# From which SBUF pool the operand tiles of the down projection's products come

## The chip, the cores and the metric

The kernel runs on one core of a Trainium2 chip. The metric is the device time of one execution in microseconds (us); the forecast and the result go by the median of several runs. One further execution was recorded by the hardware profiler, and all views of the profile come from it.

## What is computed

One decoder block over 1,024 tokens of width 1,024 in float32: three attention branches and their merge, then a squared-ReLU MLP. The change lies in the MLP's second product, the way down:

```python
h2 = rmsnorm(x, g_mlp_norm[l])
u = jax.nn.relu(jnp.einsum('bsd,df->bsf', h2, w_ff_up[l]))     # 1024 x 4096
x = x + jnp.einsum('bsf,fd->bsd', u * u, w_ff_down[l])         # 4096 -> 1024, the way down
```

## The kernel before

**Precision.** Each float32 operand is split into a high part (a copy rounded to the type of TensorE's operands, made by ACT) and a low part (the rest, by a subtraction on DVE). A product of two operands is three matmuls: high by high, high by low, low by high.

**The way down, lines 2509 to 2692.** The product of 1,024 x 4,096 by 4,096 x 1,024 is done by a scheme of seven block products in place of eight (`DOWN`: P1, P2, P6, P7, P5, P4, P3). The inner dimension comes in four groups of 4 x 128 pairs; the seven products of each group make 28, numbered k = 0 to 27 in `plan`. The left-hand operand of a product (128 partitions x 4 x 512) has been written to DRAM by the way up (`s_scr`) and is loaded into a "ur" tile by `load_s`. The right-hand one is a block of `w_down` (tiles w11, w12, w21, w22, loaded by `load_wb`) or a difference of such blocks (t1 to t4), taken on DVE by `right_sum`.

Each product k has 48 matmuls of 128 x 128 by 128 x 512 (line 2660): four token tiles t, four slices c, three passes. In a pass the left-hand operand is the stationary one (`sop[k]`: `sh`, `sl`) and the right-hand operand the moving one (`top[k]`: `th`, `tl`). Of the eight banks of PSUM, products of kind P1, P6, P5 and P3 use four (tags pp, pp, pp, pv), the others four (sc, sc, tr, tr).

**Order of the work.** It is written out by hand in the loop of line 2652; nothing reorders it. While product k runs, the operands of k+1 are made: behind the matmuls of t = 0 the right-hand sum and high part (`right(k+1, 0)`, ACT line 2575), behind t = 1 the right-hand low part (DVE) and the left-hand high part (`left(k+1, 0)`, ACT line 2588), behind t = 2 the left-hand low part (DVE). Between them stand the additions of finished PSUM banks to the output tiles (`out_evict`; on DVE, in group 0 partly ACT copies, line 2645). `load_s(k + 2)` and the next group's weight loads go out on SP's queue. DVE's `tensor_tensor` is called in the helper `tt`, line 1919, so all its rows have that line; tiles tell them apart.

**Pools.** A tile of 4 x 512 float32 numbers takes 8,192 bytes of each partition. Pool `RA` stands on the right-hand side of SBUF and has four places with the tag "h" (and one each of g0 to g3, which hold w21, w12, w22 and w11). Pool `V` stands on the left-hand side and has six places with the tag "sop", three with "ur" and one for each of t1 to t4. A pool hands out the places of a tag in turn, and whoever writes a place again waits for the last reader of the tile that was there. `operand(RA)` (line 1945) takes two h places, `vt("sop", F32R)` one sop place. In the program as laid out, the h places begin at byte 163,712 + 8,192 n of each partition, n = 0 to 3, and the sop places at 42,752 + 8,192 n, n = 0 to 5.

Before the change, product 0 has all four operand tiles in h places (`pieces["u"]`, `pieces["w"]`, made at the end of the way up), product 1 all four in sop places, and each later product its right-hand pair in h and its left-hand pair in sop. `parts` (line 2563) makes the operands of product 2 in two halves.

Of the kernel before, what the change touches and what calls it, by code (L numbers as in the profile page):

```python
# [15 lines left out]
F32R = mybir.dt.float32r  # L16
# [22 lines left out]
def f32(ap):  # L39
    return ap.bitcast(F32)  # L40
# [3 lines left out]
def tile_hybrid_block(  # L44
# [260 lines left out]
    RA = Pool("ra", side="right", h=4, g0=1, g1=1, g2=1, g3=1)  # L305
# [1553 lines left out]

    OUT = ("P1", "P2", "P6", "P5", "P3", "P7", "P4")  # L1860
    left, right, ring = {}, {}, {}

    def wtile(tag, dt):
# [54 lines left out]
    def tt(out_, a_, b_, op):  # L1918
        nc.vector.tensor_tensor(out_, a_, b_, op)  # L1919
# [25 lines left out]
    def operand(pool, tag="h"):  # L1945
        return tuple(pool.t(tag, [P, 4, 512], F32R) for _ in range(2))

    xm = []
    for s in range(0, ST, 2):
        t = RA.t("h", [P, 2, D])  # L1950
# [93 lines left out]
    with tc.manual_schedule():  # L2044
# [288 lines left out]
        def parts(hi, lo, raw):  # L2333
            yield Op("ACT", act_time(1024), lambda: nc.scalar.activation(hi, raw, AF.Copy))
            yield Op("DVE", dve_time(1024), lambda: tt(lo, raw, f32(hi), ALU.subtract))
# [182 lines left out]
        def vt(tag, dt=F32):  # L2518
            if tag in side_of:
                return RA.t(side_of[tag], [P, 4, 512], dt)  # L2520
            return laid.pop(tag) if tag in laid else V.t(tag, [P, 4, 512], dt)
# [4 lines left out]
        wb, sraw, sop, top = {}, {}, {}, {}  # L2526

        def load_wb(j, tag, queue_=nc.sync):
            if j < len(groups):
                p, n_ = groups[j]  # L2530
                wb[j, tag] = vt(tag)[:, :n_]
                rows = w_down[2 * p * P:2 * (p + n_) * P, :].rearrange("(c i p) n -> i p c n", i=2, p=P)
                dh = int(tag[2]) - 1
                queue_.dma_start(wb[j, tag], rows[int(tag[1]) - 1][:, :, dh * 512:(dh + 1) * 512])

        def load_s(k, queue_=nc.sync):
            if k < len(plan):
# [3 lines left out]
                r0 = (DOWN.index(kind) * NP + p) * P  # L2541
                queue_.dma_start(sraw[k], s_scr[r0:r0 + n_ * P, :].rearrange("(c p) n -> p c n", p=P))

        def right_sum(k):

            j, kind = plan[k]
            n_ = groups[j][1]
            if kind == "P6":
                r = wb[j, "t2"] = vt("t2")[:, :n_]
                tt(r, wb[j, "w22"], wb[j, "t1"], ALU.subtract)  # L2550
            elif kind == "P7":
                r = wb[j, "t3"] = vt("t3")[:, :n_]
                tt(r, wb[j, "w22"], wb[j, "w12"], ALU.subtract)
                load_wb(j + 1, "w12")
            elif kind == "P4":
                r = wb[j, "t4"] = vt("t4")[:, :n_]
                tt(r, wb[j, "w21"], wb[j, "t2"], ALU.subtract)
                load_wb(j + 1, "w21")
            else:
                r = wb[j, {"P1": "w11", "P2": "w21", "P5": "t1", "P3": "w22"}[kind]]  # L2560
            return r
# [5 lines left out]
        def right(k, part):  # L2567
            j, kind = plan[k]
            n_ = groups[j][1]
            if part == 0:  # L2570
                raw = right_sum(k)
                h_, l_ = operand(RA) if k > 1 else (vt("sop", F32R), vt("sop", F32R))
                top[k] = h_[:, :n_], l_[:, :n_], raw
                for cs in parts(k):
                    nc.scalar.activation(top[k][0][:, cs], raw[:, cs], AF.Copy)  # L2575
            else:
                h_, l_, raw = top[k]
                for cs in parts(k):
                    tt(l_[:, cs], raw[:, cs], f32(h_[:, cs]), ALU.subtract)
                if kind == "P3":  # L2580
                    load_wb(j + 1, "w22")

        def left(k, part):
            n_ = groups[plan[k][0]][1]
            if part == 0:
                sop[k] = vt("sop", F32R)[:, :n_], vt("sop", F32R)[:, :n_]
                for cs in parts(k):
                    nc.scalar.activation(sop[k][0][:, cs], sraw[k][:, cs], AF.Copy)  # L2588
            else:
                for cs in parts(k):  # L2590
                    tt(sop[k][1][:, cs], sraw[k][:, cs], f32(sop[k][0][:, cs]), ALU.subtract)
# [60 lines left out]
        for k, (j, kind) in enumerate(plan):  # L2652
            n_ = groups[j][1]
            for t in range(4):
# [9 lines left out]
                if k == 1 and t == 2:  # L2664
                    left(k + 1, 1)
# [4 lines left out]
                if k + 1 < len(plan):  # L2670
                    if t == 0:
                        right(k + 1, 0)
                    elif t == 1:
                        right(k + 1, 1)
                        left(k + 1, 0)
                    elif t == 2 and k != 1:
                        left(k + 1, 1)
# [46 lines left out]
```

## Time and profile before

| | |
|---|---|
| median of 3 runs | 1685.87 us (1685.17 to 1685.92) |
| the profiled execution | 1685.24 us |
| its span, first to last instruction | 1683.5 us |
| granted TensorE clock | 1.0 |
| way down: first weight load of product 0 to first of product 27 | 1366.10 to 1667.88 us |
| DVE, one operation on 128 x 2048 there | 2.29 us |
| ACT, one copy of 128 x 2048 there | 1.9 us |

In the views, PE is TensorE's matmuls and PEld its weight loads, DVE VectorE, ACT ScalarE, POOL GpSimd and SP the queue of SyncE. Tiles go by their tags: `pp<-h,sop` is a matmul into a bank pp with an h tile as moving and a sop tile as stationary operand. The weight load of a matmul begins about when the matmul before it begins; a matmul's own duration in the records (some 390 ns) is longer than its distance to the next, since matmuls overlap, so the pace is read from the distance of starts. The row that joins n weight loads gives the time from the start of the first to the end of the last.

### The profile page before, as it was taken

Reading aid. Unit: us, or ns where it says so; the run is one execution under the profiler, and the core shown is the slowest. Engines: PE = TensorE matmul, PEld = TensorE weight load, DVE = VectorE, ACT = ScalarE, POOL = GpSimd, SP = SyncE. Lnnn points to the kernel's source line nnn. Section 1 sums busy time; section 2 is a strip of 40 time slices with the busy share of each in tenths; the row PEclk is TensorE's granted clock in tenths of the full one; section 3 lists DMA queues with packets and bytes.
Section 4 is the critical chain, followed back from the end, with each engine's and each line's share of the span. In section 5 each row is a group of like instructions: output and inputs, shape, how many; then the busy total and the mean of one; then the engine's idle time right before and its main releaser. Section 6 shows DMA issues by size and latency. Waiting matters only on the chain.

```text
span 1683.5 us, 25003 instructions
## 1 busy us (share of the span) xinstructions
PE 1672.9 (99%) x9118; PEld 1431.8 (85%) x9118; DVE 1292.8 (77%) x2079; ACT 848.8 (50%) x1474; POOL 255.1 (15%) x440
## 2 busy tenths in 40 slices
PE   9999999999999999999999999999999999999999
PEld 9998899998888888888888887878888888888887
DVE  7977778855459888877877898987777776688775
ACT  6455555535458888876761446432333344332331
POOL 0000000000153142254400011022111120000000
PEclk9999999999999999999999999999999999999999
DMA  6445434467374354477747542144443485553532
GB/s 245 156 152 179 153 118 145 139 196 254 117 241 147 128 172 150 134 243 223 234 147 244 180 167 101 55 160 155 156 151 137 151 300 183 201 204 138 198 125 76
DMA packets 142221, 284.32 MB, mean 169 GB/s; under 512 B 16913, under 2 KB 53329, under 8 KB 142098
## 3 DMA queue, kind: packets, MB, share of 16 engines
q1 hardware_dynamic: 110562, 183.08, 31.8%
q0 software_dynamic: 31536, 99.64, 18.8%
q8 instruction: 72, 1.18, 0.3%
q14 instruction: 51, 0.42, 0.1%
HBM read 189.83 MB, written 92.83 MB: 168 GB/s over the span
## 4 chain that ended last, share of the span: by engine, by line
PE 93%; DVE 4%; DMA 1%; ACT 1%; issue 1%; SPq 0%; DVEq 0%; ACTq 0%
PE pp L1458 11%; PE pp L1146 10%; PE pp L1983 10%; PE pp L2660 8%; PE sc L1458 7%; PE sc L1146 6%; PE sc L1983 5%; PE sc L2660 4%; PE tr L2660 4%; PE tr L919 4%; PE pv L1458 3%; PE pv L2660 3%; PE tr L1983 2%; PE sc L936 2%; PE pp L936 2%; DVE h L1919 1%
## 5 line engine op out<-in xcount | busy, mean ns | idle before, releaser
L1057 DVE TENSOR_TENSOR wlo<-raw,whi 128x1024 fp32r<-128x1024 f32 (+1 forms) x88 | 107.5, 1221 | 80.4 <-ACT whi L1056 80.1
L1056 ACT ACTIVATE whi<-raw 128x1024 fp32r<-128x1024 f32 (+1 forms) x88 | 93.2, 1059 | 78.8 <-PE pp L1458 32.7
L2660 PE MATMUL pp<-h,sop 128*128 128x512 f32 x540 | 128.4, 395 | 0.0
L2660 PEld LDWEIGHTS pp<-h,sop 128*128 128x128 f32 x540 | 101.4, 188 | 24.6
L1983 PE MATMUL pp<-h,oh 128*128 128x512 f32 x384 | 120.6, 395 | 0.7 <-ACT cu L2068 0.6
L926 DVE TENSOR_TENSOR ptl<-tr,pth 128x512 fp32r<-128x512 f32 (+1 forms) x160 | 99.1, 628 | 24.1 <-ACT pth L924 23.4
L924 ACT ACTIVATE pth<-tr 128x512 fp32r<-128x512 f32 (+1 forms) x160 | 87.4, 557 | 34.8 <-PE sc L936 15.4
L1983 PEld LDWEIGHTS pp<-h,oh 128*128 128x128 f32 x384 | 72.1, 188 | 18.4 <-ACT cu L2068 1.5
L2575 ACT ACTIVATE h<-t 128x2048 fp32r<-128x2048 f32 (+1 forms) x17 | 30.8, 1815 | 109.4 <-DVE t L1919 96.6
L1375 POOL DMA_DIRECT2D raw<-w_in x32 | 24.2, 755 | 396.2 <-DVE wlo L1057 396.2
L1458 PE MATMUL pp<-h,whi 128*128 128x512 f32 x248 | 77.7, 394 | 0.0
L1146 PE MATMUL sc<-h,whi 128*128 128x512 f32 (+1 forms) x254 | 77.1, 387 | 0.0
L1983 PE MATMUL pp<-h,ol 128*128 128x512 f32 x192 | 75.8, 395 | 0.0
L1458 PE MATMUL pp<-whi,h 128*128 128x256 f32 x384 | 72.1, 283 | 0.0
L845 DVE TENSOR_TENSOR_SCAN e<-r,e 128x384 f32<-128x384 f32 (+3 forms) x64 | 66.3, 1044 | 7.0 <-ACT e L830 6.6
L1976 ACT ACTIVATE oh<-raw 128x512 fp32r<-128x512 f32 x64 | 39.4, 624 | 62.0 <-DVE raw L1919 62.0
L2660 PE MATMUL sc<-h,sop 128*128 128x512 f32 x264 | 63.4, 395 | 0.0
L2660 PE MATMUL tr<-h,sop 128*128 128x512 f32 x264 | 63.4, 395 | 0.0
L1919 DVE TENSOR_TENSOR sop<-ur,sop 128x2048 fp32r<-128x2048 f32 (+1 forms) x28 | 61.8, 2209 | 1.7 <-ACT sop L2588 1.7
L919 PE MATMUL tr<-ident,e 128*128 128x128 f32 x416 | 62.5, 273 | 0.0
L1458 PEld LDWEIGHTS pp<-whi,h 128*128 128x128 f32 x384 | 60.4, 189 | 0.0
L2660 PEld LDWEIGHTS tr<-h,sop 128*128 128x128 f32 x264 | 49.6, 188 | 12.0
(558 smaller groups left out, 5085.0 us busy)
## 6 DMA issues: line engine op xcount, KB each, us to landing
ur<-s_scr SPq DMA_DIRECT2D x26, 1024.0 KB
raw<-w_in POOLq DMA_DIRECT2D x42, 512.0 KB, 5.0
raw<-w_up SPq DMA_DIRECT2D x60, 256.0 KB
s_scr<-s POOLq DMA_DIRECT2D x60, 256.0 KB, 2.6
g<-w_down SPq DMA_DIRECT2D x14, 1024.0 KB
s_scr<-cu POOLq DMA_DIRECT2D x48, 256.0 KB, 2.8
h<-sbk_scr POOLq DMA_DIRECT2D x64, 128.0 KB, 3.0
o<-gate_scr SPq DMA_DIRECT2D x32, 256.0 KB
```

The lines of the kernel that those rows point to most:

```text
L845: nc.vector.tensor_tensor_scan(out=back, data0=rho[:, :u][:, ::-1], data1=back, initial=0.0 if last else beta[:, c + u:c + u + 1], op0=ALU ...
L919: nc.tensor.transpose(tr[:, jj * 256 + a * P:jj * 256 + (a + 1) * P], es[a][:, j * P:(j + 1) * P], ident)
L924: yield Op("ACT", act_time(512 - lo_c), lambda: nc.scalar.activation(ph[:, lo_c:], tr[:, lo_c:], AF.Copy))
L926: yield Op("DVE", dve_time(512 - lo_c), lambda: nc.vector.tensor_tensor(pl[:, lo_c:], tr[:, lo_c:], f32(ph[:, lo_c:]), ALU.subtract))
L936: nc.tensor.matmul(pv[0][:, c_:256], pair.v[:, j, b, :], p_[:, jj * 256 + c_:(jj + 1) * 256], start=(k == 0 and n_ == 0 and i == 0), stop= ...
L1056: yield Op("ACT", 0.03 + act_time(m), lambda: nc.scalar.activation(hi, raw, AF.Copy))
L1057: yield Op("DVE", dve_time(m), lambda: nc.vector.tensor_tensor(lo, raw, f32(hi), ALU.subtract))
L1146: nc.tensor.matmul(ps, a_, b_, start=(first and i == 0), stop=(last and i == n - 1))
L1458: nc.tensor.matmul(out_, a_, b_, start=(first and n == 0 and j == 0), stop=(last and n == 3 and j == len(todo) - 1), skip_group_check=True)
L1919: nc.vector.tensor_tensor(out_, a_, b_, op)
L1983: nc.tensor.matmul(ps, w[a_][:, k * P:(k + 1) * P], h[b_][k], start=(first and k == 0 and i == 0), stop=(last and k == 3 and i == 2), skip ...
L2660: nc.tensor.matmul(ps, a_[:, c, qs], b_[:, c, :], start=(kind in ("P1", "P2", "P7") and c == 0 and i == 0), stop=(kind in ("P2", "P4", "P3 ...
```

## The change

A helper `pair(k)` gives two tiles: from sop places if k is odd, from h places if it is even. Both operands of product k now take their tiles from it. So the even products from 2 on have all four operand tiles in h places and the odd ones all four in sop places. Products 0 and 1 stay as they were, and no instruction is added, left out or moved.

```diff
+        def pair(k):
+            return (vt("sop", F32R), vt("sop", F32R)) if k % 2 else operand(RA)
+
         def right_sum(k):
...
                 raw = right_sum(k)
-                h_, l_ = operand(RA) if k > 1 else (vt("sop", F32R), vt("sop", F32R))
+                h_, l_ = pair(k)
                 top[k] = h_[:, :n_], l_[:, :n_], raw
...
             if part == 0:
-                sop[k] = vt("sop", F32R)[:, :n_], vt("sop", F32R)[:, :n_]
+                sop[k] = tuple(t[:, :n_] for t in pair(k))
                 for cs in parts(k):
```

## The prediction

> **What bounds the kernel now.** I read the page first, for the engine that carries the span.
>
> ```profile
> span 1683.5 us, 25003 instructions
> PE 1672.9 (99%) x9118; PEld 1431.8 (85%) x9118; DVE 1292.8 (77%) x2079; ACT 848.8 (50%) x1474; POOL 255.1 (15%) x440
> PE 93%; DVE 4%; DMA 1%; ACT 1%; issue 1%; SPq 0%; DVEq 0%; ACTq 0%
> ```
>
> PE is busy for 99% of the span and makes up 93% of the chain that ended last. The change touches only the last stage (matmuls of line 2660, 28 products of 48 matmuls), so I asked next for the busy time of each engine over stretches cut at the first weight loads of products 0, 1, 2, 3, 4 and 27. Columns: stretch, its length, then busy time and instructions of each engine, the granted clock, DMA share, GB/s.
>
> ```profile
> 1366.10:1377.01 10.91, 10.91 (x50) 9.02 (x49) 8.46 (x8) 3.64 (x5) 5.16 (x9) 1.00 0.75 273
> 1377.01:1387.89 10.88, 10.88 (x49) 9.01 (x48) 9.05 (x7) 4.50 (x5) 0.00 (x0) 1.00 0.95 351
> 1387.89:1399.08 11.19, 11.19 (x49) 9.01 (x48) 9.21 (x7) 5.17 (x5) 0.00 (x0) 1.00 0.73 261
> 1399.08:1410.28 11.20, 11.20 (x49) 9.01 (x48) 7.53 (x5) 6.01 (x6) 0.56 (x1) 1.00 0.52 195
> 1410.28:1667.88 257.60, 257.60 (x1105) 207.24 (x1104) 194.16 (x156) 88.40 (x51) 1.64 (x3) 1.00 0.46 160
> ```
>
> In every stretch PE's busy time equals the stretch: PE never stands still in this stage, and the view of who waited for whom has no row that begins with PE between 1366 and 1684 us. So no wait can be taken away here; the stage gets shorter only if a matmul itself gets faster. The clock is 1.00 throughout. Yet the products are not equally long: 10.91 and 10.88 us, then 11.19 and 11.20. The weight loads in order of time show which tiles go with which length (start, length, engine, line, bank <- moving, stationary tile, count):
>
> ```profile
> 1366.10 8.14 PEld L2660 LDWEIGHTS pp<-h,h 128*128 128x128 f32 x36
> 1374.29 2.68 PEld L2660 LDWEIGHTS pv<-h,h 128*128 128x128 f32 x12
> 1377.01 5.41 PEld L2660 LDWEIGHTS sc<-sop,sop 128*128 128x128 f32 x24
> 1382.45 5.40 PEld L2660 LDWEIGHTS tr<-sop,sop 128*128 128x128 f32 x24
> 1387.89 8.34 PEld L2660 LDWEIGHTS pp<-h,sop 128*128 128x128 f32 x36
> 1396.28 2.75 PEld L2660 LDWEIGHTS pv<-h,sop 128*128 128x128 f32 x12
> 1399.08 5.55 PEld L2660 LDWEIGHTS sc<-h,sop 128*128 128x128 f32 x24
> 1404.68 5.55 PEld L2660 LDWEIGHTS tr<-h,sop 128*128 128x128 f32 x24
> ...
> 1667.88 8.35 PEld L2660 LDWEIGHTS pp<-h,sop 128*128 128x128 f32 x36
> 1676.28 2.75 PEld L2660 LDWEIGHTS pv<-h,sop 128*128 128x128 f32 x12
> ```
>
> Product 0 reads all four operands from h tiles, product 1 all four from sop tiles: 24 weight loads in 5.40 us. From product 2 on, the right-hand (moving) operand is h and the left-hand (stationary) one sop: 24 loads in 5.55, 36 in 8.35 instead of 8.14, and so to the end. From 1387.89 to 1667.88 lie 25 products, 279.99 us, 11.20 each or 233.3 ns a matmul; product 1 has 10.88 / 48 = 226.7 ns. The two fast products are the two that do already what the change makes all others do.
>
> **What could make the 6.6 ns.** Not the bank: pp, pv, sc and tr all have both paces. Not the first write of a bank: product 3 starts its sums afresh in sc and tr and takes 11.20. Not a lighter load beside PE: product 1 has the highest DMA share (0.95) and DVE busy for 9.05 of 10.88 us, product 3 has 0.52 and 7.53 of 11.20. What is left is where the operands lie. By the program's own layout the h tiles lie at byte 163,712 + 8,192 n of a partition, the sop tiles at 42,752 + 8,192 n: two tiles of a pool lie a whole number of 8,192 bytes apart, an h and a sop tile never do (120,960 is 14 times 8,192 and 6,272 over; the remainder by 256 is 128). In products 0 and 1 the stationary tile lies above the moving one in some passes and below it in others (by +16,384, -8,192, +8,192 and by +32,768, -8,192, +24,576), all at one pace, so neither the order nor the distance of the tiles in the pool matters. Only that both are of one pool, or, what comes to the same here, that they lie alike against 256 bytes.
>
> **The change part by part.** *The pace of products 2 to 27.* Even ones become h,h in the four tiles of product 0, odd ones sop,sop. Products 0 and 1 together took 1387.89 - 1366.10 = 21.79 us, 10.895 each, the step from one pool to the other included, which now comes at every product. Now 26 x 11.20 = 291.2 us; then 26 x 10.895 = 283.3; saved 7.9. By product 1 alone (10.88) it would be 26 x 0.32 = 8.3. I take 8.0; it is all on the path, since PE has no gap in which to lose it.
>
> A page of the Trainium skill speaks against this: "SBUF — State Buffer", section "Who interferes with whom", has it that TensorE reads weights and moving operand through two independent ports and never waits on anyone, so the tiles' places would be worth 0 and the time 1685.9. This trace differs with it at 226.7 against 233.3 ns, and the measurement decides; what remains of the rule is the first rival below.
>
> *Instructions and transfers.* No ACT, DVE, PE or DMA instruction is added or taken away, each keeps its place in its queue, and the loads on SP's queue wait for the same ur and weight tiles: 0.
>
> *Tile reuse, even products.* Left-hand tiles had six sop places for two a product, free after product k-3; now four h places, free after product k-2. The wait would stand on ACT (left-hand high part, line 2588), with PSUM copies behind it while group 0 runs, and DVE's low part behind that. But ahead of it on ACT stands the right-hand high part (line 2575) of the same product, which waits already today for product k-2:
>
> ```profile
> ACT h L2575 <- PE pv L2660: 47.3, 9, 7.5
> ACT h L2575 <- PE tr L2660: 22.4, 3, 7.5
> ```
>
> These are its waits, nine and three times, for the last bank of a product. When it has passed, the left-hand tiles are free as well: 0. What cannot be excluded is a later semaphore, bounded by nothing below zero and some tenths of a us above, on an operand that is ready early anyway.
>
> *Tile reuse, odd products.* They take four of six sop places, so the right-hand high part needs only product k-4 and its waits go. What is late next is DVE's low part, which stands in DVE's queue behind the PSUM additions of the running product: 0 again, as PE waits for neither.
>
> *Is DVE in time at the new pace?* Over the long stretch DVE is busy 194.16 of 257.60 us, 75%; at 10.895 a product it is 77%. What counts is the last operand, the left-hand low part, which the third matmul of a product loads. The tightest places are the ends of product 2 and of product 8:
>
> ```profile
> 1390.37 2.29 DVE L1919 TENSOR_TENSOR t<-g,g 128x2048 f32<-128x2048 f32 x1
> 1394.64 2.29 DVE L1919 TENSOR_TENSOR h<-t,h 128x2048 fp32r<-128x2048 f32 x1 [1.98 <-ACT h L2575]
> 1396.92 2.29 DVE L1919 TENSOR_TENSOR sop<-ur,sop 128x2048 fp32r<-128x2048 f32 x1
> ```
> ```profile
> 1453.32 2.28 DVE L1919 TENSOR_TENSOR t<-g,g 128x2048 f32<-128x2048 f32 x1
> ...
> 1463.85 2.28 DVE L1919 TENSOR_TENSOR sop<-ur,sop 128x2048 fp32r<-128x2048 f32 x1
> ...
> 1466.28 8.35 PEld L2660 LDWEIGHTS pp<-h,sop 128*128 128x128 f32 x36
> ```
>
> End of product 2: the low part is ready at 1396.92 + 2.29 = 1399.21; product 3 begins to load at 1399.08, its third load comes two matmuls later, 1399.55: 0.34 us of cover. This chain starts from product 1's late loads, which do not move, while product 2 gets 0.31 shorter: 0.03 left. Cost between 0 and, with a semaphore's delay, about 0.3, once; I take 0. End of product 8: ready at 1466.13, third load at 1466.28 + 0.47 = 1466.75, cover 0.62. The chain hangs on the additions of product 7's third quarter; up to the end of product 8 one and a quarter products get shorter, 0.39: 0.23 left, cost 0. If every end of a P2 product (1, 8, 15, 22) cost 0.5 us, that were 2.0: the upper bound that I use.
>
> **Sum.** The profiled execution took 1685.24 us, 1.74 of it outside its span; less 8.0 it is 1677.2, with a span of 1675.5. The median of the runs is 0.63 above that execution, and the forecast goes by the median: 1685.87 - 8.0 = **1677.9 us**.
>
> **The rivals.** *Places don't matter*: products 0 and 1 are fast because they come first, and the others stay at 11.20: 1685.9 us. For it: the trace has just two such products, both at the start. Against it: the step at 1387.89 comes exactly with the tiles, under more DMA than later. Chance 0.03.
>
> *Only placements like those of products 0 and 1 are fast.* The odd products step through six sop places by fours, so only 7, 13, 19 and 25 repeat product 1's tiles exactly; 13 even ones and these 4 gain 17 x 0.305 = 5.2: 1680.7 us. Against it: three distances in each of products 0 and 1, of both signs, at one pace. Chance 0.05.
>
> *Slower: the lost third buffer.* If the left-hand tiles of even products were free only after product k-1, high and low part (1.91 on ACT, 2.29 on DVE) would lie wholly behind it, and PE would stand for 4.2 us at 13 places: 54.6 - 8.0, 1732 us. It decides from 8.0 / 13 = 0.6 us of idle time at each such place. The ACT row is:
>
> ```profile
> 1436.40 1.91 ACT L2588 ACTIVATE sop<-ur 128x2048 fp32r<-128x2048 f32 x1
> ```
>
> For it: h has four places and an even product now takes all four. Against it: product k-1 is odd and reads none of them. Chance 0.02. That the change does not do what it says I see no room for: `pair` draws both halves of a product from one pool at every k.
>
> **How the numbers follow.** My forecast has 0.90. The range takes in the bounds of its terms: the lowest run less the largest gain, 1685.17 - 8.3 = 1676.9, with a little for a lower run 1676.7; and on the other side 1685.92 - 8.0 + 2.0 = 1679.9, so 1680.0. The rivals stay outside with 0.10 together. About 0.2% (3.4 us) is what a measurement of this kernel can tell from no change. The forecast and the partial gain (5.2) are faster by more: 0.95; the first rival is within it: 0.03; the lost buffer is slower: 0.02.
>
> **What would show each step.** Right: the weight-load rows of line 2660 read h,h for even and sop,sop for odd products, each 24 near 5.41 us and 36 near 8.15; the products begin 10.9 us apart; PE's busy time still equals every stretch; nothing before 1387.89 has moved; the wait of ACT for PE at line 2575 stays for even products and goes for odd ones. Wrong: sop,sop products of two lengths (the second rival); all products at 11.2 (the first); or gaps of PE ahead of even products, with ACT at line 2588 waiting for PE (the third). A gap at the start of product 3 alone would be the DVE chain that I put at 0.

## The result and the profile after

| | before | after |
|---|---|---|
| median | 1685.83 us (6 runs, 1684.14 to 1687.31) | 1677.78 us (6 runs, 1677.32 to 1679.12) |
| ratio after / before, 95% interval | | 0.9954 [0.9941, 0.9967] |
| profiled execution, its span | 1685.24, 1683.5 us | 1677.32, 1675.5 us |

The forecast was 1677.9 us with a span of 1675.5. The interval of the ratio means a gain of 5.6 to 9.9 us, so that the medians agree with the forecast more closely than they can tell; the trace measures the gain better. The head of the page:

```profile
span 1675.5 us, 24997 instructions
PE 1665.9 (99%) x9118; PEld 1432.9 (86%) x9118; DVE 1292.2 (77%) x2079; ACT 849.0 (51%) x1474; POOL 255.2 (15%) x440
PE 91%; DVE 4%; ACT 1%; issue 1%; DMA 0%; DVEq 0%; ACTq 0%
```

PE's busy time fell by 7.0 us with the same 9118 matmuls. DVE's and ACT's moved by 0.6 us at most. So no work went away: matmuls became quicker. (The span fell by 8.0. The other 1.0 us is no gain of the change: up to 1357 us PE was 1.0 us less idle and 1.0 us longer busy than before, and the way down began at the same time.) The stretches of the way down, cut as before at the first weight loads of products 0, 1, 2, 3, 4 and 27:

```profile
1366.14:1377.05 10.91, 10.91 (x50) 9.02 (x49) 8.54 (x9) 3.63 (x5) 5.16 (x9) 1.00 0.76 287
1377.05:1387.93 10.88, 10.88 (x49) 9.01 (x48) 9.04 (x7) 4.51 (x5) 0.00 (x0) 1.00 1.01 382
1387.93:1398.83 10.90, 10.90 (x50) 9.02 (x49) 8.86 (x7) 5.18 (x5) 0.00 (x0) 1.00 0.59 213
1398.83:1409.73 10.90, 10.90 (x49) 9.01 (x48) 7.81 (x5) 6.01 (x6) 0.56 (x1) 1.00 0.55 210
1409.73:1660.20 250.47, 250.47 (x1105) 207.33 (x1104) 193.90 (x156) 88.27 (x51) 1.64 (x3) 1.00 0.48 165
```

The first two rows are the old ones to within 0.01 us, and the stage begins at 1366.14 instead of 1366.10: nothing ahead of it has moved. Products 2 and 3 now take 10.90, and the 23 products from 1409.73 to 1660.20 take 250.47 us, 10.89 each; before it were 257.60 and 11.20. The weight loads in order of time carry the tiles beside the lengths:

```profile
1387.93 8.13 PEld L2663 LDWEIGHTS pp<-h,h 128*128 128x128 f32 x36
1396.11 2.68 PEld L2663 LDWEIGHTS pv<-h,h 128*128 128x128 f32 x12
1398.83 5.43 PEld L2663 LDWEIGHTS sc<-sop,sop 128*128 128x128 f32 x24
1404.30 5.40 PEld L2663 LDWEIGHTS tr<-sop,sop 128*128 128x128 f32 x24
...
1660.20 8.13 PEld L2663 LDWEIGHTS pp<-sop,sop 128*128 128x128 f32 x36
1668.38 2.68 PEld L2663 LDWEIGHTS pv<-sop,sop 128*128 128x128 f32 x12
```

Both kinds of product run at the pace that products 0 and 1 had all along: 24 loads in 5.40, 36 in 8.13. What is not yet told is which property of the tiles does it, since the change alters two together: the pool, and the position.

### The profile page after: what moved, and what is told of

It is laid out like the page before. It is cut to its first block, busy times and chain, and to the rows that moved or that the text cites. A ratio compares the mean times of both kernels' runs of the same rounds, so it can differ in the third digit from the quotient of the medians.

```text
span 1675.5 us, 24997 instructions
## 1 busy us (share of the span) xinstructions
PE 1665.9 (99%) x9118; PEld 1432.9 (86%) x9118; DVE 1292.2 (77%) x2079; ACT 849.0 (51%) x1474; POOL 255.2 (15%) x440
## 4 chain that ended last, share of the span: by engine, by line
PE 91%; DVE 4%; ACT 1%; issue 1%; DMA 0%; DVEq 0%; ACTq 0%
PE pp L1458 11%; PE pp L1983 10%; PE pp L1146 9%; PE pp L2663 8%; PE sc L1458 7%; PE sc L1146 6%; PE sc L1983 5%; PE tr L2663 4%; PE sc L2663 4%; PE tr L919 4%; PE pv L1458 3%; PE pv L2663 3%; PE tr L1983 2%; PE sc L936 2%; PE pp L936 2%; DVE h L1919 1%
## 5 line engine op out<-in xcount | busy, mean ns | idle before, releaser
L2663 PE MATMUL pp<-h,h 128*128 128x512 f32 x288 | 66.6, 389 | 0.0
L2663 PE MATMUL pp<-sop,sop 128*128 128x512 f32 x288 | 66.6, 389 | 0.0
L2663 PEld LDWEIGHTS pp<-h,h 128*128 128x128 f32 x288 | 54.1, 188 | 11.3
L2663 PEld LDWEIGHTS pp<-sop,sop 128*128 128x128 f32 x288 | 54.1, 188 | 11.3
L919 PEld LDWEIGHTS tr<-ident,e 128*128 128x128 f32 x416 | 50.6, 140 | 10.0
L1977 DVE TENSOR_TENSOR ol<-raw,oh 128x512 fp32r<-128x512 f32 x64 | 43.1, 688 | 16.8 <-ACT oh L1976 16.8
L1458 PEld LDWEIGHTS pp<-h,whi 128*128 128x128 f32 x248 | 46.7, 189 | 11.0
```

The lines of the kernel that those rows point to most:

```text
L919: nc.tensor.transpose(tr[:, jj * 256 + a * P:jj * 256 + (a + 1) * P], es[a][:, j * P:(j + 1) * P], ident)
L1458: nc.tensor.matmul(out_, a_, b_, start=(first and n == 0 and j == 0), stop=(last and n == 3 and j == len(todo) - 1), skip_group_check=True)
L1977: nc.vector.tensor_tensor(l_, src, f32(h_), ALU.subtract)
L2663: nc.tensor.matmul(ps, a_[:, c, qs], b_[:, c, :], start=(kind in ("P1", "P2", "P7") and c == 0 and i == 0), stop=(kind in ("P2", "P4", "P3 ...
```

## The experiments

Those on the way down compare it over the same stretch, from the first weight load of product 4 to that of product 27, 23 products; the rows are the stretch, its length, PE and PEld busy with their counts, the clock, DMA share and GB/s. Lengths per product are these lengths by 23. The stretch is used, and not the span, because the start of the way down lies between 1365.7 and 1369.0 us among programs that are alike up to there.

**Shifting one pool.** The kernel before, with an unused tile of 128 bytes at the bottom of pool V:

```diff
-        V = Pool("v", sop=6, ur=3, t1=1, t2=1, t3=1, t4=1)
+        V = Pool("v", pad=1, sop=6, ur=3, t1=1, t2=1, t3=1, t4=1)
...
+        V.t("pad", [P, 32])
         laid = {tag: V.t(tag, [P, 4, 512], F32R if tag == "sop" else F32)
```

> The kernel before, with an unused tile of 128 bytes laid ahead of the tiles of pool V: the pools of each operand are as before (h and sop mixed from product 2 on), but the sop places now lie like the h places against 256 bytes. Theory 'position against 256 bytes': every product takes 10.88 us, and since two neighbouring products also lie alike, the step of 0.01 us between products goes: span 1675.2 us, 8.3 us (0.5%) faster than before. Theory 'the pool (or the side of SBUF) decides': products 2 to 27 stay at 11.20, span 1683.5. Theory 'the gain comes from writing the next operands into the other pool than the one read': as little changed, 1683.5.

```profile
1411.35:1661.61 250.26, 250.26 (x1106) 207.26 (x1105) 1.00 0.47 165
```
```profile
1389.14 8.12 PEld L2661 LDWEIGHTS pp<-h,sop 128*128 128x128 f32 x36
1397.30 2.68 PEld L2661 LDWEIGHTS pv<-h,sop 128*128 128x128 f32 x12
```

10.88 us a product, with h and sop still mixed in every one: 36 loads in 8.12 where the kernel before has 8.34 for the same two kinds of tile. The median is 1678.53 us over 5 runs, 0.9955 [0.9941, 0.9968] of the kernel before. So neither the pool, nor the side of SBUF, nor writing into the other pool than the one read is what gains; the position is. The rival theories of the pool and of the writes are refuted by this one program. (The pad also moves pool V's other tiles, ur and t1 to t4; in the changed kernel these stay where they were, and the pace is the same, so they are not the cause.) The span was 1676.9 instead of 1675.2, since the stage began 1.3 us later and product 3 took 11.33 us, 0.45 more than the others, because of a gap, for which see below.

The same 128 bytes in the changed kernel:

> The changed kernel with the same 128 bytes ahead of the tiles of pool V. All operands of all products lie alike against 256 bytes, within a product and from one to the next. Theory 'position': 10.88 us a product in place of 10.89, the two longer distances at each change of pool (232 and 231 ns) become 227, span 1675.2. Theory 'pool': the change of pool still costs 0.01 us, span 1675.5.

```profile
1409.96:1660.20 250.24, 250.24 (x1105) 207.21 (x1104) 1.00 0.47 165
```

10.88 instead of 10.89: the step at each change of pool is gone too, though the pools still change. The span stayed at 1675.5 all the same: the stage began at 1365.73, 0.41 us earlier than in the changed kernel, and the other products gained some 0.25 us, but product 3 took 11.57 us in place of 10.90:

```profile
1398.39 0.41 PEld L2664 LDWEIGHTS sc<-sop,sop 128*128 128x128 f32 x2
1399.59 4.90 PEld L2664 LDWEIGHTS sc<-sop,sop 128*128 128x128 f32 x22 [0.78 <-DVE sop L1919]
```
```profile
1380.87 2.29 DVE L1919 TENSOR_TENSOR t<-g,t 128x2048 f32<-128x2048 f32 x1 [1.94 <-DMA g<-w_down]
...
1397.24 2.29 DVE L1919 TENSOR_TENSOR sop<-ur,sop 128x2048 fp32r<-128x2048 f32 x1
```

Two weight loads, then 0.78 us without one until DVE's low part is ready at 1397.24 + 2.29 = 1399.53. Two things make it late: the low part came 0.28 us later than in the changed kernel, since in product 1 DVE waited 1.94 us for a load of w_down (1.31 there), and product 3 was to begin 0.44 us earlier. This is the third weight load of product 3, the place at which the prediction had 0.03 us left.

**How finely the position counts.** The pad with 64 bytes, and then with 32, 96 and 192:

> The kernel before, with 64 bytes in place of 128 ahead of the tiles of pool V: the remainder between an h and a sop place by 256 is now 64 or 192. Theory 'position': if any remainder but zero costs the same, products 2 to 27 at 11.20 us and the span at 1683.5; if the cost goes by how much of two blocks of 128 bytes falls together, half of it, 11.04 us a product and 1679.4. Products 0 and 1 at 10.9 in either case. Theory 'pool': 1683.5. Theory 'any shift of pool V helps': 1675.2.

> The kernel before with 32 bytes ahead of the tiles of pool V: an h and a sop place differ by 160 or 96 against 256 bytes (128 in the kernel before, 0 with 128 bytes, 192 or 64 with 64). Theory 'the cost falls with what the two have in common of 256 bytes': between 11.20 and the 10.99 measured with 64 bytes, some 11.10 us a product. Theory 'it matters only whether the halves of 128 bytes meet, meet in part, or not at all': 10.99 as with 64 bytes.

> The same with 96 bytes: the remainder is 224 or 32. Theory 'common part': between the 10.99 of 64 bytes and the 10.88 of 128, some 10.93. Theory 'halves': 10.99.

> The same with 192 bytes: the remainder is 64 or 192, the mirror of 64 bytes. Theory 'common part' and theory 'halves': 10.99 us a product as with 64 bytes. If the direction matters, another value.

In this order:

```profile
1412.09:1664.79 252.70, 252.70 (x1106) 207.34 (x1105) 1.00 0.46 163
```
```profile
1412.21:1669.81 257.60, 257.60 (x1106) 207.23 (x1104) 1.00 0.46 160
```
```profile
1410.78:1668.38 257.60, 257.60 (x1105) 206.93 (x1104) 1.00 0.46 160
```
```profile
1410.55:1668.15 257.60, 257.60 (x1106) 207.55 (x1104) 1.00 0.46 160
```

Each of these four programs ran once. 10.99 us with 64 bytes, which no theory had foreseen, and 11.20 with 32, 96 and 192. The theory of the common part fails (96 should have been better than 64), and so does that of the halves. What stands is narrower: of the offsets tried, only lying alike gives the full pace; every other one costs, most of them the whole 0.32 us, one a third of it. Why 64 bytes cost less than their mirror 192 is open.

**One tile of four in the other pool.** The changed kernel, with one of the four operand tiles of each product from 2 on taken from the other pool. For the left-hand low part:

```diff
+        def one(k):
+            return vt("sop", F32R) if k % 2 else RA.t("h", [P, 4, 512], F32R)
...
+        def split(k):
+            return (one(k), one(k + 1)) if k > 1 else pair(k)
...
-                sop[k] = tuple(t[:, :n_] for t in pair(k))
+                sop[k] = tuple(t[:, :n_] for t in split(k))
```

The high parts go by `(one(k + 1), one(k))`, the right-hand operand in `right` in the same way.

> The changed kernel, but from product 2 on the low part of the left-hand operand alone (stationary in the third pass) is taken from the other pool. Theory 'each matmul whose own two operands lie differently costs 6.7 ns more': one of three passes, 0.107 us a product, 26 x 0.107 = 2.8 us, span 1678.3. Theory 'a matmul and the weight load beside it act on each other', by runs of matmuls with the same arrangement in other stages of the kernel before (13 ns per three passes): 26 x 0.213 = 5.5, span 1681.0.

> The same with the low part of the right-hand operand alone (moving in the second pass) from the other pool. Theory 'own operands': one of three passes, span 1678.3. Theory 'neighbours', by the same arrangement in other stages (20 ns per three passes): as much as with all mixed, 26 x 0.32 = 8.3, span 1683.8.

> The same with the high part of the right-hand operand alone (moving in the first and third pass) from the other pool. Theory 'own operands': two of three passes, 26 x 0.213 = 5.5, span 1681.0. Theory 'neighbours', by the same arrangement in other stages (7 ns per three passes): 26 x 0.107 = 2.8, span 1678.3.

> The same with the high part of the left-hand operand alone (stationary in the first and second pass) from the other pool. Theory 'own operands': two of three passes, span 1681.0. Theory 'neighbours', by the same arrangement in other stages (20 ns per three passes): span 1683.8.

In this order:

```profile
1410.41:1665.94 255.53, 255.53 (x1106) 208.72 (x1105) 1.00 0.47 162
```
```profile
1389.73:1400.73 11.00, 11.00 (x50) 9.01 (x49) 1.00 0.62 217
...
1412.16:1667.09 254.93, 254.93 (x1106) 207.34 (x1105) 1.00 0.47 162
```
```profile
1412.90:1666.13 253.23, 253.23 (x1105) 207.06 (x1104) 1.00 0.47 163
```
```profile
1410.97:1668.18 257.21, 257.21 (x1106) 207.40 (x1104) 1.00 0.47 161
```

| tile in the other pool | us a product | theory "own operands" | theory "neighbours" |
|---|---|---|---|
| none (the changed kernel) | 10.89 | | |
| left-hand low | 11.11 | 10.99 | 11.10 |
| right-hand low | 11.08 (product 2: 11.00) | 10.99 | 11.20 |
| right-hand high | 11.01 | 11.10 | 11.00 |
| left-hand high | 11.18 | 11.10 | 11.20 |

Each arrangement ran once. The columns of the theories are 10.89 with 0.107, 0.213 or 0.32 added. Those of "neighbours" are no derivation from a mechanism: they carry over what the same arrangement costs in other stages of the kernel before. "Own operands" misses all four, and in the wrong order: the right-hand high part, which is off in two passes of three, costs least. "Neighbours" hits three within 0.02, which shows that the cost of these arrangements is the same from stage to stage, and not why. The fourth, the right-hand low part, it misses: there the same arrangement runs at 11.00 in product 2, the only one at that pace, and at 11.08 to 11.09 from product 4 on, so that the arrangement alone does not set the pace; what else does was not tested. So one misplaced tile in four takes from over a third to nearly all of the gain. A rule that gives the cost of every arrangement was not found.

**The same rule in other stages.** If the position is the cause, it must pay wherever operands lie differently. The way up (line 1983 in the kernel before) multiplies tiles of pools RA and RB with tiles of pool M. The changed kernel, with 128 bytes at the bottom of M:

```diff
-    M = Pool("m", raw=8, oh=8, ol=8, cu=8)
+    M = Pool("m", pad=1, raw=8, oh=8, ol=8, cu=8)
+    M.t("pad", [P, 32])
```

> The changed kernel with an unused tile of 128 bytes laid ahead of the tiles of pool M, which holds the stationary operands (oh, ol) of the way up. Of its 1344 matmuls of line 1983, 1152 read a moving operand of pool RA or RB, whose places differ by 128 from M's against 256 bytes in the kernel as changed, and alike with the 128 bytes; of the other 192, with pool W, 128 change from alike to different and 64 the other way. Theory 'position': 1152 x 6.7 ns = 7.7 us at most, less some 0.4 to 0.9 for those of W: 7 us faster than the changed kernel, span near 1668.5; less where those matmuls wait for operands. Theory 'pool': nothing, since the pools stay what they were, 1675.5.

The median of 5 runs was 1673.64 us, 0.9932 [0.9918, 0.9945] of the kernel before. The matmuls' durations (least, median, most, then first and last start), in the changed kernel and with the pad:

```profile
L1983 PE MATMUL pp<-h,oh x384: 387/393/505, 1069.4 to 1363.1; 128*128 128x512 f32 x192
```
```profile
L1984 PE MATMUL pp<-h,oh x384: 387/389/504, 1070.4 to 1359.0; 128*128 128x512 f32 x192
```

The median goes from 393 to 389 ns, as between mixed and pure products, and the same matmuls run from 1070.4 to 1359.0, 288.6 us in place of 293.7: 5.1 saved of the 7 expected. One us was lost ahead of this stage (1070.4 against 1069.4; the runs do not show to what), and product 3 of the way down gave back 0.7. The span was 1671.9, so 3.6 us of the 7 arrived.

To this was added the same alignment in pool W, whose places are 4,224 bytes apart, an odd multiple of 128, so that high and low parts always lay differently. Weights of 1,024 columns now begin 0 or 128 bytes into their place:

```diff
+    starts = {id(t): (i // 2 + j) % 2 for i, pair in enumerate(WP.free) for j, t in enumerate(pair)}
+
+    def wv(t, m, want=1):
+        o = 32 if m <= 1024 and starts[id(t)] != want else 0
+        return t[:, o:o + m]
...
-                views = tuple(w_[:, :1024].rearrange("p (k n) -> p k n", k=4) for w_ in pair)
+                want = int(kind not in ("P6", "P7", "P5"))
+                views = tuple(wv(w_, 1024, want).rearrange("p (k n) -> p k n", k=4) for w_ in pair)
```

> The same, and in pool W the weights of 1024 columns begin 0 or 128 bytes into their place, so that they lie against 256 bytes like the tile that they are multiplied with (all matmuls of lines 1146 and 1458 with pools RA, T, T4 and MT; before, high and low part always lay differently, so one of them was off). Theory 'position': those with 512 columns stand at some 231 to 233 ns and go to 227: 1560 x 5.5 = 8.6 us; those with 256 columns stand near 119 and could go to 113: some 1440 x 6 = 8.6 us; where TensorE waits for operands nothing is saved, so 8 to 17 us beyond the 7 of pool M: span 1651 to 1661. Theory 'pool': 1675.5.

The median of 4 runs was 1668.73 us, 0.9898 [0.9885, 0.9912] of the kernel before: the fastest version here, though its span of 1666.8 misses the forecast of 1651 to 1661. Pool W gave 5.1 us in place of 8 to 17. Matmuls of the input projection with 512 and with 256 columns, in the changed kernel and in this one:

```profile
L1458 PE MATMUL pp<-whi,h x384: 274/282/368, 195.2 to 365.1; 128*128 128x256 f32 x192
...
L1458 PE MATMUL pp<-h,whi x248: 389/395/404, 116.3 to 481.8; 128*128 128x512 f32 x124
```
```profile
L1464 PE MATMUL pp<-whi,h x384: 278/283/365, 192.9 to 364.4; 128*128 128x256 f32 x192
...
L1464 PE MATMUL pp<-h,whi x248: 389/389/398, 115.8 to 478.4; 128*128 128x512 f32 x124
```

With 512 columns the median falls from 395 to 389 ns. With 256 columns it goes from 282 to 283: nothing is gained there, and between 190 and 360 us this line has 1321 matmuls in place of 1325, so that the 8.6 us expected of them are missing. Most of what was expected of line 1146 (L1151 in this version) is missing too, although all its 512-column matmuls of pool RA with W now lie alike:

```profile
L1146 PE MATMUL pp<-g,whi x160: 387/393/477, 86.6 to 741.7; 128*128 128x512 f32 x160
```
```profile
L1151 PE MATMUL pp<-g,whi x160: 387/393/478, 86.0 to 738.0; 128*128 128x512 f32 x160
```

The median stays at 393. In the program 132 of these 160 stand in threes or sixes between matmuls with other operands. Where 48 matmuls of this line follow one another without a break, the distance of starts falls from 233 to 227 ns; a group of three takes 699 ns in the changed kernel and 701 here. So it is not enough that a matmul's own two operands lie alike; why the short groups gain nothing was not tested.

The way up shows the gain of pool M's pad as a count: in the same 167 us 736 matmuls in place of 721, here as with the pad alone.

```profile
1190.00:1357.00 167.00, 167.00 (x721) 135.55 (x721) 1.00 0.44 157
```
```profile
1190.00:1357.00 167.00, 167.00 (x736) 137.66 (x734) 1.00 0.49 167
```

## Why the prediction was right, point by point

*The bound.* That PE never stands still in the way down, so that only quicker matmuls help, held: the trace after has no wait of PE between 1366 and 1676 us either, and the whole gain is in the pace. Products 2 to 26 took 279.99 us and now take 272.27, 7.72 less; product 27 with the end gives another 0.32.

*The pace.* 10.895 us a product was forecast, from products 0 and 1; 10.89 came. The step between pools, which the forecast included, is there, and with the pad, which lays both pools alike, it vanishes (10.88): it comes from the position too.

*What lies behind it.* The prediction left open whether the pool or the position against 256 bytes counts, having argued from two products that the order and distance of the tiles do not; the ten different placements of products 2 to 27, all at 10.89 to 10.91 us, bear that out. The shifted pool decides for the position. That 256 is the measure, and not 512, is borne out by the last kernel: in its program 360 of the 840 512-column matmuls of the input projection (L1464) have operands an odd multiple of 256 bytes apart, and all groups of that line's 512-column matmuls are down to 389 ns in the median all the same.

*The rule of the Trainium skill* ("SBUF — State Buffer", "Who interferes with whom") that TensorE's two reads are independent and never wait on anyone would have given no change. The runs differ with it: where moving and stationary tiles lie differently against 256 bytes, a matmul with its weight load takes up to 3% longer (233.3 against 226.7 ns). Whether one read waits for the other there, the runs do not show.

*Tile reuse.* The right-hand high part of odd products no longer waits for PE, as forecast, and that of even ones still does, four times (26.1 us). One wait came that the prediction did not list. ACT's waits in the way down:

```profile
ACT h L2578 <- PE pv L2663: 17.1, 3, 9.0
...
ACT sop L2591 <- PE pv L2663: 13.4, 5, 5.4
ACT h L2578 <- PE tr L2663: 9.0, 1, 9.0
...
ACT sop L2591 <- PE tr L2663: 5.3, 1, 5.3
```

With the right-hand part of odd products gone ahead, the left-hand one (line 2591, sop) now waits for product k-2, six times and 18.7 us together. DVE waited once for a left-hand high part (2.3 us), and PE for nothing, so it costs nothing; the prediction had named DVE's low part alone as next in line.

*DVE in time.* The low part for product 3 was ready at 1396.96 + 2.29 = 1399.25:

```profile
1394.67 2.29 DVE L1919 TENSOR_TENSOR sop<-t,sop 128x2048 fp32r<-128x2048 f32 x1 [2.04 <-ACT sop L2578]
1396.96 2.29 DVE L1919 TENSOR_TENSOR sop<-ur,sop 128x2048 fp32r<-128x2048 f32 x1
```

Product 3 began to load at 1398.83 and took 5.43 for its first 24 loads instead of 5.41: the cover was indeed just used up. But the bound of 0.3 us for this place, put down to a semaphore's delay that no run shows by itself, was too small, as the versions with a pad show: product 3 lost 0.45 us in one and 0.7 in others. The bound took the loads of w_down to come at the same moment against the matmuls in each run, and they do not. The loss stayed within the 2.0 us that the range allowed for such places. The other tight place, the end of product 8, stayed without loss, with less cover than the 0.23 us forecast: its low part was ready at 1464.52, and product 9 began to load at 1464.18, its third load some 0.45 later.

*The rivals.* "Places don't matter" and "only placements like those of products 0 and 1" fell with the first result: each product from 4 to 26 takes 10.89 us. The second was priced wrongly, though. It took the places to come round strictly in turn, and in the program as laid out they do not: only products 8, 13, 16, 24 and 25 repeat the places of product 0 or 1 exactly, not 17 of them. By that rival 5 x 0.305 = 1.5 us would have been saved, not 5.2. That the 21 other placements have the full pace as well refutes it the more clearly. No gap came ahead of even products.

## What to carry to other kernels

Where TensorE is busy without a gap, compare the pace of like matmuls that differ only in where their operands lie: two paces in one stage are a gain to be had without touching the schedule. Lay all operands of an unbroken stage of 512-column matmuls alike against 256 bytes, high and low parts too; here 128 unused bytes at the bottom of a pool did the same as drawing all tiles from one pool, and places of an odd multiple of 128 bytes prevented it. Then look at the operands that were ready only just in time, for they are late next.

## What the runs showed of the hardware that was not expected

- A 512-column matmul with its weight load takes 226.7 ns when moving and stationary tiles lie alike against 256 bytes (10.88 us for 48) and 233.3 when the moving one's place less the stationary one's leaves 32, 96, 128 or 192 bytes (11.20), whatever pools they come from; where it leaves 64 it is 229 (10.99). This holds for an unbroken stream in which all moving tiles have the one place against 256 bytes and all stationary tiles the other. The runs do not show the mechanism.
- With 256 columns lying alike gained nothing: 282 and 283 ns in the median. Nor did it with 512 columns where the matmuls stand in groups of three between others: some 700 ns a group in both versions.
- The cost is not the sum over matmuls of their own two operands: one misplaced tile of four costs from 0.12 us a product (right-hand high, off in two passes) to 0.29 (left-hand high, off in two passes).
- With one misplaced tile (right-hand low), products of the same arrangement ran at 11.00 and at 11.08 us in the same execution.
